# Weight casts moved to GpSimd inside attention's steps, with two weight loads ordered behind the queries' transfers

## Chip, cores and metric

The kernel runs on one core of one Trainium2 chip. The metric is the device time of one execution in microseconds; the time before is the median of three executions.

## What is computed

A trunk of two decoder layers over one sequence of 512 tokens, width 1024, in float32. Layer 0 mixes tokens in chunks of 128 with a gated MLP; then one shared key/value projection is made. Layer 1 is sliding-window attention over these keys and values, with 16 query heads of 64 in 4 groups, a linear distance bias and a learned sink per head. Each layer is followed by a gated MLP of width 2816 with a causal convolution of width 3 and by a gated embedding. The part around the change is this:

```python
q = (xn @ w_q).reshape(B, nb, BLOCK, N_KV_HEADS, GQA_GROUP, HEAD_DIM)
scores = einsum('bnikgd,bnjkd->bnkgij', q, kblk) * (HEAD_DIM ** -0.5)
scores = scores - slopes[:, :, None, None] * dist
scores = where(valid[None, :, None, None], scores, -inf)
m = maximum(max(scores, axis=-1, keepdims=True), sink)
e = exp(scores - m)
probs = e / (sum(e, axis=-1, keepdims=True) + exp(sink - m))
out = einsum('bnkgij,bnjkd->bnikgd', probs, vblk)
return out.reshape(B, S, N_Q_HEADS * HEAD_DIM) @ w_o
```

`kblk` and `vblk` hold, for each block of 128 queries, the previous and the current block of 128 keys.

## The kernel before, in words

Activations lie transposed, features on partitions and tokens along the row. Every float32 product with a weight is made of three matmuls on rounded halves: high x high, high x low, low x high (`mm3`, lines 181 to 183). So each weight is split before use. `plan` writes down the weights in the order of use as *pieces*; a piece of 2048 columns has two *units* of 1024. `load` (line 129) issues a piece's DMA on SyncE's queue into a raw buffer. `pump` makes units ready: ScalarE rounds the raw unit into the high half `wh` (line 154), VectorE subtracts it from the raw one into the low half `wl` (line 155). Both halves have four buffers (`WBUFS`), so a unit's cast waits until TensorE has read the unit four places earlier. During attention there is one raw buffer (`state["tags"] = [0]`), so a piece's load waits for the subtraction of the piece before.

The order of the pieces here is: half of the key/value weight, query weight 0, the other half, query weights 1 to 3, output weights 0 to 3, and then the second MLP.

Attention runs in 16 steps, group g of heads by block n of queries, as a pipeline over a loop `i`: `scores(i)`, the filling work of the step (`fill`), `mix(i-2)`, `turn(i-1)`, `weights(i)`.

- `scores` (lines 774 to 793): two matmuls per head give the scores; VectorE folds the two key blocks with a predicated copy (784) and reduces them with the bias to an exponent and its extreme (788); GpSimd puts the sink into the last column (774); ScalarE takes the four exponentials and their sums (793).
- `weights` (801 to 807): VectorE's reciprocal; one head is scaled by VectorE (807), three by ScalarE (805).
- `turn` (822, 252, 253, 830): TensorE transposes the four heads, ScalarE and VectorE split the result into halves, and GpSimd's affine selects keep the part that belongs to the previous block.
- `mix` (844 to 857): the products with the values; ScalarE and VectorE add the two halves, ScalarE rounds the output (856), GpSimd subtracts for its low half (857).
- `fill` takes from the table `beside`: in steps 0 to 9 the projections of query groups 1 to 3 (`project`), then parts of the output projection (`merge`), and in some steps `more`, which pumps one unit ahead. Steps 0, 1, 3, 4, 6, 7, 10 and 11 have it.

`queries` scales a projected group, splits it (ScalarE at 657, VectorE at 658) and, for the groups 1 to 3, moves the halves into place with four DMAs on SyncE's queue (661, 662), as each half of the partitions has to hold the other side's data.

The order of instructions on each engine is the framework's: a scheduler takes them by priority as they become ready in its own estimate, with `scores`, `turn` and `weights` at high priority. Engines and DMA queues then work strictly in that order. So an instruction that waits holds back what stands behind it on its engine.

Of the kernel before, what the change touches and what calls it, by code (L numbers as in the profile page):

```python
# [8 lines left out]
F32 = mybir.dt.float32  # L9
# [39 lines left out]
def tile_yoco(ctx: ExitStack, tc: tile.TileContext, t, out: bass.AP, out_b: bass.AP):  # L49
    nc = tc.nc  # L50
# [14 lines left out]
    pieces, paired = [], set()  # L65

    def plan(ap_, n, cols, own=None):

        if own and len(own) > 1:
            m = n // len(own)  # L70
            cuts = [(q * m, m) for q in range(len(own))]
        else:
            m = n if n <= UNIT else (n // cols + 1) // 2 * cols
            cuts = [(0, m), (m, n - m)] if m < n else [(0, n)]
        pieces.append((ap_, n, cuts, own))

    def plan_cols(w, n_chunks, kk, cols=256, k0=0):
        for c in range(n_chunks):
            plan(w[c, :, k0 * cols : (k0 + kk) * cols], kk * cols, cols)
# [6 lines left out]
    def plan_ffn(l):  # L86
        for i, (j0, j1) in enumerate(PARTS):
            if i == 0:
                plan_cols(t["w_up"][l], j1, KD)
            else:  # L90
                plan_cols(t["w_up"][l, j0 + 1 : j1], j1 - j0 - 1, KD)
            if i + 1 < len(PARTS):
                plan_cols(t["w_up"][l, j1 : j1 + 1], 1, KD)
            else:
                plan(t["pT"][l], 2 * S, S, own=[(mp, "m4", "m5")])
                plan_cols(t["w_pin"][l], 2, 4)
            plan_cols(t["w_down"][l], 4, j1 - j0, k0=j0)
# [9 lines left out]
    plan_cols(t["w_q"][0:1], 1, KD)  # L107
    plan_cols(t["w_kv"][1:2], 1, KD)
    plan_cols(t["w_q"][1:4], 3, KD)
    plan_cols(t["w_o"], 4, KD)  # L110
    plan_ffn(1)
    free = [j % SLOTS for j in range(NJ, NJ + 8)]
# [4 lines left out]

    units = [(i, q, lo, n) for i, p in enumerate(pieces) for q, (lo, n) in enumerate(p[2])]
    raws, ready = {}, {}
    state = {"raw": 0, "unit": 0, "next": 0, "tags": [0, 1, 2], "turn": 0, "pt": 0}  # L120

    def load(upto, queue=nc.sync):
        while state["raw"] < min(upto, len(pieces)):
            j = state["raw"]
            a, m = pieces[j][:2]
            tags = state["tags"]
            r = wp.tile([P, 2 * UNIT], F32, tag=f"r{tags[state['turn'] % len(tags)]}", bufs=1, name=f"wraw{j}")
            state["turn"] += 1
            queue.dma_start(r[:, :m].rearrange("p (c m) -> p c m", c=2) if j in paired else r[:, :m], a)
            raws[j] = r  # L130
            state["raw"] += 1

    def pump(upto):
        while state["unit"] < min(upto, len(units)):
            i, q, lo, n = units[state["unit"]]
            load(i + 1)
            u = state["unit"]
            own = pieces[i][3]
            if own:
                pool, *tags = own[q]  # L140
                wh, wl = (pool.tile([P, n], F32R, tag=tg, name=f"own{u}_{tg}") for tg in tags)
            else:
                wh = wp.tile([P, UNIT], F32R, tag="wh", bufs=WBUFS, name=f"wh{u}")
                wl = wp.tile([P, UNIT], F32R, tag="wl", bufs=WBUFS, name=f"wl{u}")
            if i in paired:
                whole = raws[i][:, : pieces[i][1]].rearrange("p (c k n) -> p k c n", c=2, n=256)
                src = whole[:, lo // S : (lo + n) // S]
                hi, low = (x[:, :n].rearrange("p (k c n) -> p k c n", c=2, n=256) for x in (wh, wl))
            else:
                src, hi, low = raws[i][:, lo : lo + n], wh[:, :n], wl[:, :n]  # L150
            if u == 0:
                nc.vector.tensor_copy(hi, src)
            else:
                nc.scalar.copy(hi, src)  # L154
            nc.vector.tensor_sub(low, src, hi.bitcast(F32))  # L155
            ready[u] = (wh, wl, n)
            state["unit"] += 1
# [41 lines left out]
    def v(name, i):  # L199
        c = VEC[name] + i  # L200
        return vec[:, c : c + 1]
# [61 lines left out]
    class Norm:  # L263
# [25 lines left out]
        def turn(self):  # L289

            sq = tp.tile([P, S], F32, tag="sq", name=f"{self.name}turn")
            nc.vector.transpose(sq, self.acc)
            self.quarter = const.tile([P, S // 32], F32, tag="quarter", bufs=1, name=f"{self.name}quarter")
            nc.vector.tensor_reduce(self.quarter, sq.rearrange("p (b f) -> p b f", f=32),
                                    axis=mybir.AxisListType.X, op=ALU.add)
# [48 lines left out]
    def gain(name, l=0):  # L344
        return lambda k: v(name, l * KD + k)
# [215 lines left out]
    for c in range(4):  # L561
# [4 lines left out]
        for j in range(2):  # L566
            m = 2 * c + j
# [14 lines left out]
            hi = ap.tile([P, S], F32R, tag=f"ah{m}", name=f"ush{m}")  # L582
# [58 lines left out]
    def queries(ps, g, j):  # L641


        qf = tp.tile([P, S], F32, tag="sq", name=f"qf{g}_{j}")
        m = 2 * g + j
        nc.vector.scalar_tensor_tensor(qf, ps, qscale[:, m : m + 1], rstd, op0=ALU.mult, op1=ALU.mult)
        res = [tp.tile([P, S], F32R, tag=("hs", "sg", "c0", "c1")[2 * j + e], name=f"q{g}_{j}_{e}")
               for e in range(2)]
        if g == 0:
            for e, q in enumerate(res):  # L650
                me, it = sides[e], sides[1 - e]
                nc.scalar.copy(q[me, :], qf[me, :])
                nc.vector.tensor_sub(q[it, :], qf[me, :], q[me, :].bitcast(F32))
            return res

        hi = tp.tile([P, S], F32, tag="acc", name=f"qhi{g}_{j}")
        nc.scalar.copy(hi.bitcast(F32R), qf)
        nc.vector.tensor_sub(qf.bitcast(F32R), qf, hi)
        for e, q in enumerate(res):
            me, it = sides[e], sides[1 - e]  # L660
            nc.sync.dma_start(q[me, :].bitcast(F32), hi[me, :])
            nc.sync.dma_start(q[it, :].bitcast(F32), qf[me, :])
        return res

    qs = {0: []}
    for j in range(2):
        qs[0] += queries(qps[j], 0, j)
# [87 lines left out]
    def fill(i):  # L755
        for f, *args in beside.get(i, []):
            f(*args)
# [9 lines left out]
    def scores(i):  # L767


        g, n = steps[i]  # L770
        nk = 2 * P if n else P
        t0 = (n - 1) * P if n else 0
        pr = prs[:, i % 2]
        nc.gpsimd.tensor_copy(pr[:, :, P], nsink[:, GQ * g : GQ * (g + 1)])
        neg = at.tile([P, GQ], F32, tag="neg", bufs=2, name=f"neg{i}")
        for b in range(2):
            sc = psum(f"sc{i}_{b}").rearrange("p (e h k) -> p e h k", e=2, h=2)
            for j in range(2):
                o = sc[:, j].rearrange("p h k -> p (h k)")[:, :nk]
                q = qs[g][2 * b + j][:, n * P : (n + 1) * P]  # L780
                nc.tensor.matmul(o, q, kh[g // 2][:, g % 2, t0 : t0 + nk], start=True, stop=False)
                nc.tensor.matmul(o, q, kl[g // 2][:, g % 2, t0 : t0 + nk], start=False, stop=True)
            if n:
                nc.vector.copy_predicated(sc[:, :, 0, :], both(own.bitcast(mybir.dt.int32)), sc[:, :, 1, :])
            for j in range(2):
                e = 2 * b + j
                hd = GQ * g + e
                nc.vector.tensor_tensor_reduce(out=pr[:, e, :P], in0=far if n else near, in1=sc[:, j, 0, :],
                                               scale=-slope(hd), scalar=nsink[:, hd : hd + 1],
                                               op0=ALU.add, op1=ALU.min, accum_out=neg[:, e : e + 1])  # L790
        sm = at.tile([P, GQ], F32, tag="sm", bufs=2, name=f"sm{i}")
        for e in range(GQ):
            nc.scalar.activation(pr[:, e, :], pr[:, e, :], AF.Exp, bias=neg[:, e : e + 1], scale=-1.0,
                                 accum_out=sm[:, e : e + 1])
        live[i] = (pr, sm)
# [63 lines left out]
    last = len(steps)  # L859
# [2 lines left out]
    state["tags"] = [0]  # L862
    pts4 = wp.tile([P, 4, S], F32R, tag="r1", bufs=1, name="pts4")
    for i in range(last + 2):
        if i < last:
            with tc.high_priority():
                scores(i)
        if i <= last:
            fill(i)
        if i >= 2:  # L870
            mix(i - 2)
        if i > last:
            fill(i)
        if 0 <= i - 1 < last:
            with tc.high_priority():
                turn(i - 1)
        if i < last:
            with tc.high_priority():
                weights(i)
    state["tags"] = [0, 1, 2]  # L880
    nf = Norm("nf1", [(xp, "x", gain("norm_ffn", 1))])
    for c in range(4):
        for m in (2 * c, 2 * c + 1):
# [226 lines left out]
```

## Time and profile before

| | before |
|---|---|
| median of 3 executions | 1141.46 us (1141.1 to 1141.71) |
| profiled execution | 1141.22 us, of which the span is 1139.5 |
| TensorE busy | 1127.0 us (99%) |
| VectorE busy | 749.6 us (66%) |
| ScalarE busy | 530.0 us (47%) |
| GpSimd busy | 107.7 us (9%) |
| granted TensorE clock | 0.998 |
| casts of line 154 on ScalarE | 197, 202.0 us in all, 1028 ns each |

Busy shares are means over all stages; attention's steps lie between about 591 and 688 us of the span. In the timelines a row gives the start, the duration, the engine, the line, the operation with its output and inputs, and in brackets how long the engine stood idle before and who ended that. PE is TensorE, ACT ScalarE, DVE VectorE, POOL GpSimd, SPq the queue of SyncE.

### The profile page before, as it was taken

The numbers are of one execution on the slowest core, as the hardware profiler recorded it, in microseconds if no ns is written. First come the engines' busy times: TensorE is split into PE (matmuls) and PEld (weight loads), VectorE is DVE, ScalarE is ACT, GpSimd is POOL, SyncE is SP. The second block draws the span as 40 slices with busy tenths as digits, with TensorE's granted clock in tenths as the row PEclk, the third lists the DMA queues.
The fourth block names the chain that finished last, engine by engine and source line by source line (L and its number), as shares of the span: only waits on it lengthen the run. The fifth ranks groups of instructions, "written<-read, shape, count | busy, mean of one in ns | idle before, by whom it ended". The sixth has DMA issues, their size and how long they took to land.

```text
span 1139.5 us, 13604 instructions
## 1 busy us (share of the span) xinstructions
PE 1127.0 (99%) x5266; PEld 940.5 (83%) x5266; DVE 749.6 (66%) x1158; ACT 530.0 (47%) x875; POOL 107.7 (9%) x175
## 2 busy tenths in 40 slices
PE   9999999999999999999999999999999999999997
PEld 7888888888888888888898878888888888888896
DVE  7366477763677367557988977777636763675675
ACT  6533344441344234445657985444313432355562
POOL 2000200000000000021213343000000000000222
PEclk9999999999999999999999999999999999999999
DMA  8422323223223322432224315223223233224302
GB/s 298 145 83 74 111 75 111 101 85 111 78 98 102 111 76 86 134 107 79 74 75 129 93 38 185 98 88 111 78 107 110 66 102 111 93 80 160 111 1 75
DMA packets 25776, 115.41 MB, mean 101 GB/s; under 512 B 2920, under 2 KB 8176, under 8 KB 16240
## 3 DMA queue, kind: packets, MB, share of 16 engines
q1 hardware_dynamic: 25152, 113.89, 29.8%
q8 instruction: 41, 0.67, 0.2%
q10 hardware_dynamic: 560, 0.66, 0.2%
q14 instruction: 23, 0.19, 0.1%
HBM read 108.24 MB, written 2.11 MB: 97 GB/s over the span
## 4 chain that ended last, share of the span: by engine, by line
PE 95%; DVE 2%; issue 1%; ACT 1%; DMA 1%; POOL 0%; SPq 0%; POOLq 0%; DVEq 0%; ACTq 0%
PE up L181 14%; PE up L183 14%; PE up L182 14%; PE d L183 8%; PE d L181 8%; PE d L182 8%; PE gate L181 2%; PE gate L183 2%; PE gate L182 2%; PE u L182 1%; PE u L183 1%; PE u L181 1%; PE o L182 1%; PE o L181 1%; PE o L183 1%; PE q L181 1%
## 5 line engine op out<-in xcount | busy, mean ns | idle before, releaser
L154 ACT CAST wh<-wraw 128x1024 fp32r<-128x1024 f32 (+2 forms) x197 | 202.0, 1028 | 264.6 <-PE d L182 131.0
L155 DVE TENSOR_TENSOR wl<-wraw,wh 128x1024 fp32r<-128x1024 f32 (+1 forms) x198 | 238.4, 1205 | 127.9 <-ACT wh L154 127.6
L181 PE MATMUL up<-nf00h,wh 128*128 128x512 f32 x352 | 137.1, 390 | 0.0
L181 PE MATMUL up<-nf10h,wh 128*128 128x512 f32 x352 | 137.0, 389 | 0.0
L182 PE MATMUL up<-nf00l,wh 128*128 128x512 f32 x352 | 136.9, 389 | 0.0
L183 PE MATMUL up<-nf00h,wl 128*128 128x512 f32 x352 | 136.9, 389 | 0.0
L183 PE MATMUL up<-nf10h,wl 128*128 128x512 f32 x352 | 136.9, 389 | 0.0
L182 PE MATMUL up<-nf10l,wh 128*128 128x512 f32 x352 | 136.9, 389 | 0.0
L181 PE MATMUL d<-ah,wh 128*128 128x512 f32 x352 | 136.9, 389 | 0.0
L182 PE MATMUL d<-al,wh 128*128 128x512 f32 x352 | 136.9, 389 | 0.0
L183 PE MATMUL d<-ah,wl 128*128 128x512 f32 x352 | 136.9, 389 | 0.0
L379 ACT ACTIVATE c<-hs,vec 128x512 f32<-128x512 f32 x88 | 71.5, 815 | 72.0 <-DVE hs L375 71.2
L380 DVE SCALAR_TENSOR_TENSOR c<-hs,vec,c 128x511 f32<-128x511 f32 x88 | 65.8, 749 | 34.5 <-ACT c L379 34.4
L355 DVE TENSOR_TENSOR h<-h,d 128x512 f32<-128x512 f32 x56 | 38.4, 686 | 73.8 <-PE d L183 73.8
L252 ACT CAST ah<-a 128x512 fp32r<-128x512 f32 x44 | 27.4, 622 | 109.5 <-DVE a L385 109.4
L183 PEld LDWEIGHTS up<-nf10h,wl 128*128 128x128 f32 x352 | 66.1, 188 | 13.8
L182 PEld LDWEIGHTS d<-al,wh 128*128 128x128 f32 x352 | 66.1, 188 | 13.8
L183 PEld LDWEIGHTS up<-nf00h,wl 128*128 128x128 f32 x352 | 66.1, 188 | 13.8
L183 PEld LDWEIGHTS d<-ah,wl 128*128 128x128 f32 x352 | 66.1, 188 | 13.7
L182 PEld LDWEIGHTS up<-nf00l,wh 128*128 128x128 f32 x352 | 66.1, 188 | 13.7
L182 PEld LDWEIGHTS up<-nf10l,wh 128*128 128x128 f32 x352 | 66.1, 188 | 13.7
L181 PEld LDWEIGHTS d<-ah,wh 128*128 128x128 f32 x352 | 66.1, 188 | 13.6
(454 smaller groups left out, 2061.7 us busy)
## 6 DMA issues: line engine op xcount, KB each, us to landing
wraw<-in_w_up SPq DMA_DIRECT2D x44, 1024.0 KB, 4.8
wraw<-in_w_down SPq DMA_DIRECT2D x16, 896.0 KB, 4.6
wraw<-in_w_down SPq DMA_DIRECT2D x8, 1024.0 KB, 4.8
wraw<-in_w_gate SPq DMA_DIRECT2D x8, 1024.0 KB, 4.8
wraw<-in_w_u SPq DMA_DIRECT2D x4, 1024.0 KB, 5.9
wraw<-in_w_out SPq DMA_DIRECT2D x4, 1024.0 KB, 4.8
wraw<-in_w_q SPq DMA_DIRECT2D x4, 1024.0 KB, 4.9
wraw<-in_w_o SPq DMA_DIRECT2D x4, 1024.0 KB, 4.9
```

What stands on the lines that cost most here:

```text
L154: nc.scalar.copy(hi, src)
L155: nc.vector.tensor_sub(low, src, hi.bitcast(F32))
L181: nc.tensor.matmul(ps, wh[:, a:b], xh, start=st, stop=False)
L182: nc.tensor.matmul(ps, wh[:, a:b], xl, start=False, stop=False)
L183: nc.tensor.matmul(ps, wl[:, a:b], xh, start=False, stop=en)
L252: nc.scalar.copy(hi, src)
L355: nc.vector.tensor_add(h[m], h[m], ps)
L379: nc.scalar.activation(c, hs, AF.Identity, bias=v("conv_b", l * 2 * NJ + col), scale=cw[2])
L380: nc.vector.scalar_tensor_tensor(c[:, 1:], hs[:, : S - 1], cw[1], c[:, 1:], op0=ALU.mult, op1=ALU.add)
```

## The change

Inside the loop over attention's steps the function that makes the high half of a weight unit is chosen by the step: GpSimd's copy for the steps 1 to 14, ScalarE's in all others. `pump` calls whatever is set when it asks for the unit.

Also, the DMAs of a query group's second half (`j` of 1) are kept for the groups 2 and 3, and the load of the piece `outs + g - 1`, which is output weight 1 or 2, is given an edge behind them. The edge orders the instructions in SyncE's queue; it adds no semaphore.

```diff
+    outs = len(pieces)
     plan_cols(t["w_o"], 4, KD)
...
+    def behind(ins, front):
+        tc.add_manual_dep(ins.ins, front.ins.name,
+                          mybir.DependencyInfo(mybir.DependencyClass.NoSync, mybir.DependencyReason.DATA),
+                          reason="order")
...
-            queue.dma_start(r[:, :m].rearrange("p (c m) -> p c m", c=2) if j in paired else r[:, :m], a)
+            ins = queue.dma_start(r[:, :m].rearrange("p (c m) -> p c m", c=2) if j in paired else r[:, :m], a)
+            for front in state["sent"].pop(j, []):
+                behind(ins, front)
...
-                nc.scalar.copy(hi, src)
+                state["cast"](hi, src)
             nc.vector.tensor_sub(low, src, hi.bitcast(F32))
...
-            nc.sync.dma_start(q[me, :].bitcast(F32), hi[me, :])
-            nc.sync.dma_start(q[it, :].bitcast(F32), qf[me, :])
+            sent = [nc.sync.dma_start(q[me, :].bitcast(F32), hi[me, :]),
+                    nc.sync.dma_start(q[it, :].bitcast(F32), qf[me, :])]
+            if g > 1 and j:
+                state["sent"].setdefault(outs + g - 1, []).extend(sent)
...
     for i in range(last + 2):
+        state["cast"] = nc.gpsimd.tensor_copy if 0 < i < last - 1 else nc.scalar.copy
         if i < last:
...
     state["tags"] = [0, 1, 2]
+    state["cast"] = nc.scalar.copy
```

More of the change, by code (lines that the diff above doesn't have):

```diff
@@ L119, in tile_yoco @@
     raws, ready = {}, {}
-    state = {"raw": 0, "unit": 0, "next": 0, "tags": [0, 1, 2], "turn": 0, "pt": 0}
+    state = {"raw": 0, "unit": 0, "next": 0, "tags": [0, 1, 2], "turn": 0, "pt": 0, "sent": {}, "cast": nc.scalar.copy}
+    def behind(ins, front):
+        tc.add_manual_dep(ins.ins, front.ins.name,
+                          mybir.DependencyInfo(mybir.DependencyClass.NoSync, mybir.DependencyReason.DATA),
+                          reason="order")
     def load(upto, queue=nc.sync):
```

## The prediction

> **What bounds the kernel now.** I read the page first, then busy time by stretches of the attention, then the waits of TensorE and VectorE there, then the timelines of the engines around each wait, and last the chain of waits.
>
> ```profile
> span 1139.5 us, 13604 instructions
> PE 1127.0 (99%) x5266; PEld 940.5 (83%) x5266; DVE 749.6 (66%) x1158; ACT 530.0 (47%) x875; POOL 107.7 (9%) x175
> ```
>
> TensorE is busy for 1127.0 of 1139.5 us: all that any edit can return without taking matmuls away is 12.5 us, most of it at the two ends. The change acts in attention's sixteen steps, so I cut them where TensorE's idle time changes.
>
> ```profile
> core 0: us, PE busy (x) PEld busy (x) DVE busy (x) ACT busy (x) POOL busy (x), PEclk, DMA share, GB/s
> 603.00:649.50 46.50, 46.50 (x256) 39.76 (x254) 40.13 (x129) 39.99 (x126) 15.73 (x33) 1.00 0.43 123
> 649.50:662.50 13.00, 10.54 (x59) 7.77 (x58) 12.51 (x49) 12.77 (x48) 5.85 (x14) 1.00 0.25 50
> 662.50:669.50 7.00, 7.00 (x37) 5.60 (x35) 4.80 (x18) 5.87 (x20) 3.35 (x8) 1.00 0.32 135
> 669.50:684.30 14.80, 13.59 (x66) 10.55 (x66) 10.12 (x32) 10.56 (x35) 6.04 (x10) 1.00 0.00 1
> ```
>
> Up to 649.5 TensorE never stands: the queries' projections fill every step, and whatever ScalarE saves there is hidden. From 649.5 to 662.5 TensorE stands 13.00 - 10.54 = 2.46 us, with ScalarE (12.77 of 13) and VectorE (12.51) both full and GpSimd at 5.85. In the last stretch it stands 1.21 us. So 3.67 us of idle is what the change can reach. The stops in the middle stretch:
>
> ```profile
> 649.50 0.39 PE L844 MATMUL pv<-pts,vt 128*128 128x512 f32 x1
> 650.68 0.41 PE L822 MATMUL tr<-ident,prs 128*128 128x128 f32 x2 [0.80 <-DVE prs L807]
> ...
> 660.90 0.49 PE L181 MATMUL o<-oh,wh 128*128 128x512 f32 x1
> 662.11 0.50 PE L182 MATMUL o<-ol,wh 128*128 128x512 f32 x1 [0.71 <-POOL ol L857]
> ...
> PE tr L822 <- DVE prs L807: 1.7, 3, 0.8
> ...
> 652.52 0.23 PE o L181
> ```
>
> The first four rows are the first and the last stop (the bracket is the idle time and who ended it), the fifth is from TensorE's waits (us in total, times, longest), the last from the chain. That one says that a 512-wide matmul holds TensorE for 0.23 us when work follows; a bar of 0.39 contains 0.16 of draining. A stop therefore costs more from start to start than its idle time: 650.68 - 649.50 - 0.23 = 0.95 us for the first, 662.11 - 660.90 - 0.23 = 0.98 for the last. There are four: three transposes that wait for VectorE's scaling, 1.7 + 3 x 0.16 = 2.2 us together, and a projection that waits for GpSimd's low half of the output, 0.98.
>
> **The change part by part.** (a) The casts. Line 154 runs on ScalarE seven times in the steps that precede the stops:
>
> ```profile
> L154 ACT CAST wh<-wraw x7: 1032/1038/1052, 599.4 to 646.9; 128x1024 fp32r<-128x1024 f32 x7
> ...
> 642.93 0.95 ACT wh L154
> 643.90 1.23 DVE wl L155
> ```
>
> By the order in which steps ask for units, these seven are the second half of the third query weight, both halves of the fourth, and both halves of the first two output weights; all are asked for in steps 1 to 11, so all seven move. They take 0.95 us each of ScalarE's queue (the chain's row; 1.04 is the bar), 6.65 us in all. The first five lie further back under TensorE's full stretch, where nothing that ScalarE gains shows. The last two, which end at 643.9 and begin at 646.9 (1.9 us), feed the stops. The first of them is on the chain: VectorE's subtraction at 643.90 waits for it.
>
> What VectorE loses to ScalarE there, between 640 and 663, is the whole of one answer:
>
> ```profile
> DVE wl L155 <- ACT wh L154: 0.6, 1, 0.6
> DVE ds L801 <- ACT prs L793: 0.3, 1, 0.3
> DVE pts L253 <- ACT pts L252: 0.3, 1, 0.3
> DVE side L852 <- ACT side L848: 0.2, 1, 0.2
> ```
>
> 1.4 us. VectorE has no other slack before 662, so the three transposes can come earlier by at most 1.4 of their 2.2 us, however idle ScalarE becomes. I take all 1.4, because ScalarE is relieved of 1.9 us in the ten microseconds where these waits lie. The bounds are 0.6 (only the wait for the cast itself goes) and 1.4; late next is VectorE's own work.
>
> The fourth stop hangs on ScalarE and GpSimd:
>
> ```profile
> 659.68 0.60 ACT p11h L252
> 660.39 1.09 POOL pts L830
> 661.64 0.43 POOL ol L857
> ```
>
> The chain runs from ScalarE's cast of the turned probabilities, in a queue without a gap, to GpSimd. If ScalarE arrives 1.9 us sooner, less the 1.4 by which TensorE itself moved, and the select is no longer stretched by the subtraction beside it, the 0.98 goes. Bounds: 0 and 0.98; I take 0.98.
>
> What GpSimd pays: the trace has no 128x1024 cast on it. The nearest rows by width and by operation:
>
> ```profile
> L542 POOL TENSOR_SCALAR_AFFINE_SELECT wsT<-wsT 128x1024 f32<-128x1024 f32 x1 | 1.1, 1091 | 20.3 <-DMA wsT<-in_wsT 20.3
> ...
> 590.88 0.24 POOL L687 CAST diff<-vd 128x64 fp32r<-128x64 f32 x1 [16.82 <-DVE vd L708]
> 600.33 1.59 POOL L687 CAST diff<-vd 128x64 fp32r<-128x64 f32 x3 [0.41 <-DVE vd L708]
> ...
> 600.42 1.23 DVE L155 TENSOR_TENSOR wl<-wraw,wh 128x1024 fp32r<-128x1024 f32 x1
> ```
>
> Same width and one input: 1.09 us; it is the nearest, and I take it. Sixteen 64-wide casts at 0.24 would be 3.8, which counts the start sixteen times over: the upper end. Seven at 1.09 are 7.6 us on an engine that is busy for 15.73 + 5.85 + 3.35 + 6.04 = 31.0 of 81.3 us in these steps; it has room, but its queue is in order, so place matters. The last two rows show three casts that should take 0.7 taking 1.59 while VectorE subtracts weights: the two engines shut each other out. It goes the other way too:
>
> ```profile
> 540.94 1.34 POOL L282 TENSOR_TENSOR n1acc<-n1acc,n1sq 128x512 f32<-128x512 f32 x1 [4.06 <-ACT n1sq L277]
> 541.05 2.32 DVE L155 TENSOR_TENSOR wl<-wraw,wh 128x1024 fp32r<-128x1024 f32 x1
> ```
>
> A subtraction that takes 1.23 takes 2.32 behind a GpSimd instruction: up to 1.1 us per cast, taken from the very engine that bounds the stretch. [...]
>
> When would the two casts run? Each needs the buffer that the fourth query weight leaves, and the last matmuls that read its halves start at
>
> ```profile
> 640.51 0.39 PE L183 MATMUL q<-n11h,wl 128*128 128x512 f32 x1
> 645.57 0.39 PE L183 MATMUL q<-n11h,wl 128*128 128x512 f32 x1
> ```
>
> so they run from about 641 and 646. Beside the first, VectorE scales once and adds from PSUM; beside the second it reduces scores from PSUM. [...] I charge 0.2 us for both; bounds 0 and 2.2.
>
> (b) The held loads. SyncE's queue before:
>
> ```profile
> 610.91 1.10 SPq L661 DMA_DIRECT2D q<-qhi  x2
> 612.06 1.23 SPq L662 DMA_DIRECT2D q<-qf  x2
> 613.33 0.59 SPq L129 DMA_DIRECT2D wraw<-in_w_o  x1
> ...
> 631.71 1.10 SPq L662 DMA_DIRECT2D q<-qf  x2
> 633.39 0.33 SPq L129 DMA_DIRECT2D wraw<-in_w_o  x1
> ...
> 651.77 1.10 SPq L662 DMA_DIRECT2D q<-qf  x2
> 661.02 0.33 SPq L129 DMA_DIRECT2D wraw<-in_w_o  x1
> ```
>
> The two loads concerned are those at 633.39 and 661.02, and they stand behind the third and fourth queries' transfers already (631.71 and 651.77). By itself this part changes no order and costs nothing; it keeps a load, which now could be asked for sooner, from standing in SyncE's queue in front of transfers that the scores wait for. Behind each held load only later loads queue.
>
> Sum: -1.4 - 0.98 + 0.2 = -2.2 us. The profiled execution took 1141.22 us (span 1139.5 and 1.7 around it); it would be 1139.0. The median of three is 1141.46, 0.24 above it, so the forecast for the median is 1139.3. The instruction order on each engine is recomputed by the framework when costs move; the trace can't show that. It can add up to the rest of the idle time or take as much.
>
> **The rivals.** *GpSimd's queue and lock decide.* The selects of step 7 and the matmul that needs them:
>
> ```profile
> 646.42 0.64 POOL L830 TENSOR_SCALAR_AFFINE_SELECT u7l<-pts 128x512 fp32r<-128x512 f32 x1
> 647.89 0.39 PE L844 MATMUL pv<-u7l,diff 128*128 128x512 f32 x1
> ```
>
> There is 647.89 - 647.06 = 0.83 us of slack. A cast of 1.09 put in front makes it 0.3 late; one that also waits out a VectorE subtraction (0.9 more, the 600.33 row) makes it 1.1 late, and it then holds the subtraction back by 1.1. Twice, at steps 9 and 10, that is 2 x (1.1 + 1.1) = 4.4, less the 1.9 that ScalarE still gains: +2.5, or 1144.0 us. It decides from the point where cast and lock together exceed 0.83 us in front of a select. For it: VectorE is 96% full there, and a cast is longer than any GpSimd instruction now in that stretch uncontended. [...]
>
> *A load that isn't held.* The first output weight's load (613.33) is not among the held ones. It waits for the subtraction of the fourth query weight's second half, and both halves' casts now move. If they are two casts (2 x 1.09 = 2.2 us) later and the load comes to stand in front of the second query's transfers, these begin at 613.33 + 2.2 instead of 610.91, 4.6 us later, and the fifth step's scores need them. What of this the distance to that step covers I leave open: between 0 and 4.6 us, and I take the middle, 2.3, which eats the gain of 2.2: 1141.6 us (1143.9 at the upper end). Against it: the load stands 2.4 us behind those transfers now.
>
> *Nothing arrives.* VectorE takes back what ScalarE gives, or the casts and subtractions are queued just as late as now: 1141.5 us.
>
> **How the numbers follow.** About 0.2% (2.3 us) is what a measurement of this kernel can tell from no change. The forecast's mechanism gets 0.58. Its centre, 2.2, lies at that bound; reordering has more idle time left to take (3.67 and the draining, 0.16 a stop) than to give back, so I split it 0.46 faster by more, 0.12 within. GpSimd's queue gets 0.27: 0.25 slower by more and 0.02 within. The unheld load gets 0.08: its upper end 0.05 slower, its middle 0.03 within. Nothing arrives 0.07, all within. Sums: faster 0.46, same 0.24, slower 0.30. The range goes down to 4.7 us of gain (3.67 idle plus six stops' draining), 1136.8 (1141.46 - 4.7), and up to the queue's price, 1144.0; 0.05 is left out below, 0.13 above.
>
> **What would show it.** Right: seven 128x1024 casts on GpSimd near 1.1 us; no line 154 on ScalarE between 600 and 650; VectorE's waits for ScalarE between 640 and 663 near zero; TensorE's idle time before 662 down from 2.46 to about 1; the transposes' stops still for VectorE. Wrong: casts over 2 us; weight subtractions of 2 us in the steps; TensorE waiting for selects or low halves by GpSimd; scores that wait for a query's transfer; or a first stretch that is no longer full, since the whole argument takes 603 to 649.5 as closed.

## The result: slower, and by a way that the prediction had left aside

The changed kernel takes 1144.86 us (median of 7, 1144.26 to 1145.67) against 1141.10 (1141.02 to 1141.74) for the kernel before on the same chip: ratio 1.0032, 95% interval 1.0021 to 1.0042. It is 3.8 us slower. The forecast was 1139.3 us, with a range from 1136.8 to 1144.0.

The profiled execution took 1144.86 us. From the top of its page (lines carry the changed kernel's numbers from here on: the scaling, 807 before, is 818, the query's low half 667, the weight's low half 164):

```profile
span 1143.1 us, 13598 instructions
PE 1129.7 (99%) x5266; PEld 941.2 (82%) x5266; DVE 750.4 (66%) x1158; ACT 524.4 (46%) x868; POOL 118.8 (10%) x182
```

TensorE does the same 5266 matmuls and is busy for 2.7 us more than before (1129.7 against 1127.0); only the other 0.9 us of the span, longer by 3.6, is idle time. So a part of the loss lies in matmuls that run more slowly. The stretches at the same cuts as in the prediction, and one cut of their own (span, then busy time and count of each engine, the granted clock, DMA):

```profile
603.00:649.50 46.50, 46.50 (x256) 39.71 (x254) 40.73 (x129) 34.82 (x120) 25.47 (x44) 1.00 0.44 125
649.50:662.50 13.00, 9.94 (x46) 6.93 (x45) 11.44 (x44) 12.04 (x45) 6.15 (x12) 0.92 0.42 122
662.50:669.50 7.00, 7.00 (x35) 5.75 (x35) 4.90 (x16) 4.80 (x15) 2.90 (x4) 0.90 0.00 0
669.50:684.30 14.80, 13.43 (x66) 9.79 (x65) 9.83 (x36) 11.49 (x42) 6.26 (x13) 1.00 0.01 3
...
658.90:664.00 5.10, 4.99 (x16) 3.48 (x16) 3.44 (x13) 4.43 (x17) 2.43 (x7) 0.67 0.49 193
```

The first stretch is as closed as before: ScalarE has 5 us less to do there and TensorE never stands. From 649.5 to 662.5 TensorE now stands 3.06 us (2.46 before), and between 658.9 and 664.0 the granted clock is 0.67, where it was 1.00: 5.1 x 0.33 = 1.7 us of slow matmuls. About 1 us of the longer busy time is left unassigned. TensorE's waits (us in total, times, longest) and the rows behind the new one, then two rows of the kernel before:

```profile
PE tr L833 <- DVE prs L818: 1.5, 2, 0.8
PE sc L792 <- DMA q<-qf: 1.5, 1, 1.5
...
649.14 0.17 DVE L812 RECIPROCAL ds<-sm 128x4 f32<-128x4 f32 x1
649.22 1.23 DVE L164 TENSOR_TENSOR wl<-wraw,wh 128x1024 fp32r<-128x1024 f32 x1
650.38 0.47 DVE L818 TENSOR_SCALAR prs<-prs,ds 128x128 f32<-128x128 f32 x1
...
655.64 0.68 DVE L667 TENSOR_TENSOR qf<-qf,qhi 128x512 fp32r<-128x512 f32 x1
...
656.35 1.10 SPq L671 DMA_DIRECT2D q<-qf  x2
657.55 0.54 SPq L136 DMA_DIRECT2D wraw<-in_w_o  x1
...
658.68 0.30 PE L792 MATMUL sc<-kh,q 128*128 128x128 f32 x1 [1.47 <-DMA q<-qf]
```

```profile
651.06 0.68 DVE L658 TENSOR_TENSOR qf<-qf,qhi 128x512 fp32r<-128x512 f32 x1
...
659.77 1.23 DVE L155 TENSOR_TENSOR wl<-wraw,wh 128x1024 fp32r<-128x1024 f32 x1
```

Many rows stand elsewhere on VectorE than before; two catch the eye. The subtraction that makes `wl` of output weight 1's second half was at 659.77 and is now at 649.22, in front of the scaling of step 9's probabilities (steps count from 0; the expectations of g1 and g4 call it step 10's); and the query's low half, L667, was at 651.06 and is now at 655.64. Its transfer left SyncE at 651.77 and leaves now at 656.35, and step 12's scores wait 1.47 us for it. The clock falls behind that stop, which ends at 658.68: it is 1.00 up to 660.4 and 0.50 from 660.5 to 663.8.

### The profile page after: what moved, and what is told of

The parts are those of the page before. It is cut to its first block, busy times and chain, and to the rows that moved or that the text cites. A ratio compares the mean times of both kernels' runs of the same rounds, so it can differ in the third digit from the quotient of the medians.

```text
span 1143.1 us, 13598 instructions
## 1 busy us (share of the span) xinstructions
PE 1129.7 (99%) x5266; PEld 941.2 (82%) x5266; DVE 750.4 (66%) x1158; ACT 524.4 (46%) x868; POOL 118.8 (10%) x182
## 4 chain that ended last, share of the span: by engine, by line
PE 90%; DVE 4%; ACT 2%; issue 1%; POOL 1%; DMA 1%; SPq 0%; POOLq 0%; DVEq 0%; ACTq 0%
PE up L190 14%; PE up L192 14%; PE up L191 14%; PE d L191 8%; PE d L192 8%; PE d L190 8%; PE gate L190 2%; PE gate L191 2%; PE gate L192 2%; PE u L191 1%; PE u L190 1%; PE u L192 1%; PE o L191 1%; PE o L192 1%; PE o L190 1%
## 5 line engine op out<-in xcount | busy, mean ns | idle before, releaser
L163 ACT CAST wh<-wraw 128x1024 fp32r<-128x1024 f32 (+2 forms) x190 | 194.7, 1027 | 267.9 <-PE d L191 131.3
L190 PEld LDWEIGHTS up<-nf00h,wh 128*128 128x128 f32 x352 | 66.1, 188 | 13.7
```

What stands on the lines that cost most here:

```text
L163: state["cast"](hi, src)
L190: nc.tensor.matmul(ps, wh[:, a:b], xh, start=st, stop=False)
```

## The experiments

The candidates: the framework's **new instruction order** costs the time; the **casts** do, through GpSimd's queue and through the time by which GpSimd and VectorE stretch each other's instructions (2.32 us for a subtraction of 1.23 in the prediction's rows), there called the lock; the **held loads** do. Letters for theories in an expectation belong to its own round. Each kernel was timed against the kernel before on its own chip; the medians of before there lie between 1141.22 and 1141.5. So a few tenths of a microsecond between kernels of different rounds are not to be relied on.

**First round: one thing back at a time, the order free to move again.**

e1: the changed kernel, and the low half's subtraction bound ahead of that `wl`.

```
+            sub = nc.vector.tensor_sub(low, src, hi.bitcast(F32))
+            for front in state["split"].pop((i, q), []):
+                behind(sub, front)
...
+        low = nc.vector.tensor_sub(qf.bitcast(F32R), qf, hi)
+        if g == 3 and j:
+            state["split"].setdefault((outs + g - 2, 1), []).append(low)
```

> The changed kernel, with one more edge: on VectorE the subtraction that makes the second half of the second output weight's low half stands behind the subtraction that makes the last query's low half. All seven casts stay on GpSimd. Theory A (the query's subtraction was queued behind weight and step work, so its transfers left 4.6 us late and the scores waited 1.47 us, after which TensorE's clock fell): the wait for the transfer is gone, the granted clock stays 1.00 from 649.5 to 669.5, and the time is 1139 to 1141.5 us. Theory B (GpSimd's casts themselves cost it, by the lock against VectorE and by the queue in front of selects): the casts are all there, so it stays at 1144 to 1145 us.

Measured 1143.15 us, ratio 1.0014 (1.0005 to 1.0023); about half of the loss is gone, and no more; it lies in neither theory's range. The wait for the transfer is gone and the clock is at 1.00, but others have come:

```profile
PE pv L859 <- ACT prs L820: 1.4, 1, 1.4
PE tr L837 <- DVE prs L822: 1.2, 1, 1.2
PE o L192 <- ACT oh L871: 0.7, 2, 0.5
```

e2: the casts alone, no load held (`if g > 1 and j` made `if False`).

> The changed kernel without the held loads: casts on GpSimd alone. SyncE's queue then has the two output weights' loads in front of the transfers of the third and fourth queries' second halves; every other engine's order is that of the changed kernel. Theory A: the loads wait for subtractions that are over by 634.7 and 650.5, so little is lost: 1144.5 to 1146 us. If the edges on the loads are the harm, it is near 1141 us.

1144.92 us, 1.0031 (1.0019 to 1.0042): as the changed kernel, with the wait for the transfer as long (1.5 us). The held loads fall as the cause of the loss. What they are worth in the old order was not run.

e4: GpSimd casts in steps 1 to 7 only (`if 0 < i < 8`).

> The changed kernel with GpSimd's casts in steps 1 to 7 alone: five casts move, the two of the second output weight stay on ScalarE. Theory A: VectorE's order then has the query's subtraction ahead of that weight's second one, as before the change; no wait for a transfer, clock 1.00, 1140 to 1141.5 us, since the first five casts lie under a full TensorE. Theory B: five sevenths of the harm remain, about 1143.8 us.

1143.25 us, 1.0016 (1.0007 to 1.0025). VectorE's order around the query's low half is that of before, and still it is slower, with longer waits for GpSimd's `ol` (1.5 us, 0.7 before) and `oh` (0.7, 0.3 before) and a new one for `p13l` (1.0); for the scaling TensorE waits 1.7 us, as before. By its number it lies nearer to theory B; f1 below, with all seven casts on GpSimd and no loss, speaks against that theory.

e5: the changed kernel with seven 512-wide products that nothing reads in front of the waiting scores.

> The changed kernel with seven more 512-wide matmuls (0.23 us each, 1.6 in all) in front of the scores that wait for the transfer; their product is overwritten by the scores. They fill TensorE's stop and lengthen nothing else much. Theory A with the clock as a part of its own: the scores start as late as in the changed kernel, but the clock stays at 1.00 and the nine matmuls that took 0.42 us take 0.23, so about 1143 us. If the clock's fall is no consequence of that stop, or costs nothing: 1144.5 to 1145.5 us.

1144.46 us, 1.0028 (1.0018 to 1.0038), clock at 1.00. Its later waits moved as well (the scores wait 1.5 us for `p13l`), so it does not part the clock from the stop.

e1, e4 and e5 have one fault: each edit lets the framework order the steps anew, so the time mixes what was edited with another order. (e2 keeps the changed kernel's.) So the order had to be held.

**Second round: the order held.** An edge from each instruction to the one that is to be issued ahead of it on its engine fixes the order within each engine, and nothing between engines.

```
+    kept = {i.name: i for i in nc.cur_bb.bb.instructions}
+    for runs in ORDER.values():          # per engine: another kernel's order
+        names = [f"I-{n}" for a, b in runs for n in range(a, b)]
+        for front, ins in zip(names, names[1:]):
+            tc.add_manual_dep(kept[ins], front, ...)    # as in behind(): order only
```

f1 and f2 with the kernel before and the changed one make a square: order by engine of the casts.

> The seven casts stay on GpSimd and the held loads stay, but from the first k product to the last o product every engine is bound to the order of instructions that the kernel before has (779 of TensorE, 253 of VectorE, 226 of ScalarE, 101 of GpSimd, 40 of SyncE; only the casts are free to lie where GpSimd can take them). Theory A (the loss comes from the new order, not from GpSimd): at or below the kernel before, 1139.3 to 1141.5 us; no stop of TensorE for the transfer of a query, granted clock 1.00 between 649 and 670, and the stops between 649.5 and 662.5 at 2.5 us or less against 3.06 in the changed kernel. Theory B (the lock between VectorE and GpSimd, or GpSimd's queue in front of its subtractions and selects, makes the loss): 1143 us or more, with stops for VectorE's scaling or for GpSimd's ol that are longer than before's.

> The opposite corner: all casts on ScalarE as in the kernel before, the held loads in, and every engine bound to the order that the changed kernel has between the first k product and the last o product; only the seven casts are free to lie where ScalarE can take them. Theory A: the loss is there without a cast on GpSimd, 1144 to 1146 us (ScalarE's casts can add to it), with a stop of about 1.5 us for the transfer of the query behind which the clock falls. Theory B: 1141 to 1142 us.

| | casts on ScalarE | casts on GpSimd |
|---|---|---|
| order of before | 1141.22 (before) | 1140.56, ratio 0.9993 (0.9984 to 1.0002) |
| order of the changed kernel | 1145.99, 1.0045 (1.0032 to 1.0057) | 1144.86, 1.0032 (changed kernel) |

The order costs 4.8 us with the casts on ScalarE and 4.3 with the casts on GpSimd. Moving the casts gains 0.7 and 1.1 in the medians, whichever order stands; the interval of the first reaches past 1, so it is not clear of no gain. The new order is the cause, and the casts are not. f1's and f2's middle stretch:

```profile
649.50:662.50 13.00, 11.35 (x63) 8.46 (x62) 12.50 (x51) 12.66 (x48) 5.68 (x13) 1.00 0.25 52
649.50:662.50 13.00, 9.40 (x45) 6.66 (x44) 12.14 (x44) 12.53 (x47) 5.80 (x12) 0.94 0.35 96
```

f2 has the 1.5 us wait for the query's transfer and the lower clock (0.94 here, 0.87 from 662.5 to 669.5) without one cast on GpSimd.

f7 and f8 hold one engine each to the order of before and let the others follow.

> The changed kernel with VectorE alone bound to the order of the kernel before (253 instructions between the first k and the last o product); the other engines take what follows from it. TensorE's order still differs from the kernel before's at 33 places, ScalarE's at 47, GpSimd's at 8. If VectorE's order is what costs, 1141.5 us or less, and no stop for a query's transfer. If TensorE's own order costs as much as VectorE's, 1142 to 1143.5 us.

> The reverse: TensorE alone is bound to the order of the kernel before (779 instructions), VectorE's order differs from it at 88 places, ScalarE's at 87, GpSimd's at 28. If VectorE's order is what costs, 1143.5 to 1146 us with a stop for the query's transfer of 1 us or more. If TensorE's order is what costs, 1141.5 us or less.

f7: 1139.94 us, 0.9987 (0.9978 to 0.9996). f8: 1147.48 us, 1.0052 (1.0039 to 1.0064). With VectorE's order alone back the whole loss is gone, though the other engines' orders still differ from before's. f8 missed its range: TensorE's order alone back does not help. It does not price that order by itself, since the framework made yet another order for VectorE (88 places off before's). f7 first, then f8:

```profile
649.50:662.50 13.00, 12.13 (x67) 9.52 (x67) 11.84 (x46) 12.03 (x46) 6.01 (x13) 1.00 0.31 82
PE o L190 <- ACT oh L867: 0.6, 1, 0.6
PE pv L855 <- ACT prs L804: 0.5, 1, 0.5
```

```profile
649.50:662.50 13.00, 9.38 (x43) 6.91 (x42) 11.47 (x45) 11.90 (x44) 6.27 (x13) 0.88 0.42 121
PE sc L792 <- DVE neg L799: 1.9, 1, 1.9
PE tr L833 <- DVE prs L818: 1.5, 2, 0.8
```

In f7 TensorE stands 0.87 us where it stood 2.46, and its waits no longer name a scaling. f7 is also the fastest version, clear of both kernels: the change, with VectorE's order kept. f8's longest stop is for a reduction (`neg`), not for the transfer that was expected.

f6: f1 with the first five casts back on ScalarE.

> As f1_old_order, but the first five casts are back on ScalarE at the places that the kernel before gives them; only the two casts of output weight 1 are on GpSimd. If the prediction's step holds that the first five are worth nothing because TensorE has no idle time there, this is as fast as f1_old_order, 1140.3 to 1140.9 us, and its first stop for a transpose after 649 us is gone as there. If the gain comes from all seven, it is about 1141.0 to 1141.3 us.

1140.53 us, 0.9992 (0.9983 to 1.0001), against f1's 1140.56. With the order held, the five casts under the full TensorE are worth nothing that can be told from the noise, as the prediction said.

f4: f1 with rows moved by hand at two of TensorE's remaining stops.

> As f1_old_order, with two things moved by hand: in steps 9, 10 and 11 VectorE's scaling of the probabilities stands ahead of the reduction that lay between it and the reciprocal (0.24 us each), and GpSimd's subtractions for two o operands stand ahead of two selects of step 11. If TensorE's remaining stops hang on these two rows, two stops for transposes get 0.2 us shorter each and the 0.97 us stop of an o product shrinks to 0.3 us or less: 1139.3 to 1140.0 us. If the selects that are now later are waited for, the gain is eaten and it is 1140.3 us or more.

1140.04 us, 0.9988 (0.9979 to 0.9997): some 0.5 below f1, just above what was expected at best. The stop of the `o` product went from 0.97 us to 0.32 (from start to start, less the 0.23 of a product); of the two transposes one got shorter (0.78 to 0.37), the other longer (0.71 to 0.88, its own wait now for a reduction).

**Third round: single rows of VectorE's order.** Both start from f1.

> f1_old_order (casts on GpSimd, the order of the kernel before on every engine) with one row of VectorE moved to where the changed kernel has it: the 1.23 us subtraction that makes wl of output weight 1's second half stands between step 10's reciprocal and its scaling instead of 9 us later. If this row is what the new order costs, the scaling, step 10's transposes and all that VectorE does behind it come about 1.2 us later, the query's low half too: 1141.4 to 1142.4 us against 1140.6, a stop for the transposes at 649.7 of about 1 us, and a short one or none for the query's transfer. If the row is harmless by itself, 1140.3 to 1140.9 us.

> f1_old_order with the other row moved: the subtraction of the query's low half stands behind step 10's second scaling, about 4 us later, as in the changed kernel; wl stays where the kernel before has it. If the late transfer is what costs, TensorE stops for it 1 to 1.6 us in step 12's scores and the granted clock falls behind that: 1142 to 1144 us. If TensorE's other work covers it (fewer stops ahead of it than in the changed kernel), 1140.3 to 1141.5 us with the clock at 1.00; a stop of 1 us or more with the clock at 1.00 would say that the stop alone doesn't make it fall.

g1, `wl` ahead of the scaling: 1140.24 us, 0.9991 (0.9982 to 1.0000). The most conspicuous row of the new order is harmless by itself. g2, the query's low half late: 1143.21 us (1140.97 to 1145.18), 1.0017 (1.0008 to 1.0026). One row out of place costs 2.65 us over f1.

```profile
654.20 0.68 DVE L667 TENSOR_TENSOR qf<-qf,qhi 128x512 fp32r<-128x512 f32 x1
...
654.91 1.10 SPq L671 DMA_DIRECT2D q<-qf  x2
...
657.23 0.44 PE L792 MATMUL sc<-kh,q 128*128 128x128 f32 x1 [1.26 <-DMA q<-qf]
...
656.00:660.00 4.00, 2.77 (x8) 2.39 (x9) 3.69 (x16) 3.42 (x14) 1.47 (x3) 0.61 0.31 70
660.00:664.00 4.00, 4.00 (x17) 3.51 (x17) 1.69 (x4) 1.52 (x7) 0.80 (x3) 0.54 0.40 119
```

g3 puts the seven unread products into that stop, every order held.

> g2_low_late (one row of VectorE moved: the query's low half 4 us later, everything else in the order of the kernel before) with seven extra 512-wide products on TensorE, which nothing reads, in the place where it waits for the late transfer (7 x 0.23 = 1.6 us, as long as the stop). If most of what that row costs is the clock behind the stop, the clock stays at 1.00 and the time is 1140.9 to 1141.9 us, with 0.3 to 1.3 us left over f1_old_order for the stop itself. If the stop and the lateness cost it, 1142.7 to 1143.7 us as in g2_low_late, with the clock at 1.00.

1141.15 us (1140.52 to 1141.78), 0.9998 (0.9990 to 1.0007).

```profile
655.35 1.86 PE L792 MATMUL sc<-kh 128*128 128x512 f32 x7
657.05 0.22 PE L796 MATMUL sc<-kh,q 128*128 128x128 f32 x1
...
649.50:662.50 13.00, 12.27 (x69) 9.73 (x68) 11.51 (x40) 11.66 (x45) 4.77 (x12) 1.00 0.24 54
662.50:669.50 7.00, 6.79 (x36) 5.46 (x34) 5.29 (x21) 6.34 (x21) 3.19 (x8) 1.00 0.32 129
```

The scores begin as late as in g2 (657.05 against 657.23), but the clock holds at 1.00 in both stretches, where g2 has 0.78 and 0.91. Of the 2.65 us that the late row costs, 2.06 go with the clock behind the stop, and 0.59 are left for the stop and the lateness (0.42 if each kernel is taken against its own before).

g4: the changed kernel's order on all engines, with only this row back.

> The changed kernel's order on every engine, with one row of VectorE put back: the subtraction of the query's low half directly behind step 10's first scaling, some 4.6 us earlier. If that row is the larger part of the loss (2.65 us as g2_low_late has it), 1141.8 to 1142.8 us, with the clock at 1.00 and no stop for the transfer; what is left over f1_old_order, 1.2 to 2.2 us, is then the rest of the new order. If the other rows of the order cost as much again, 1143 us or more.

1145.74 us, 1.0039 (1.0026 to 1.0053): a clear miss. The wait for the transfer is gone, and another one stands 2 us further on:

```profile
660.43 0.50 PE L190 MATMUL o<-oh,wh 128*128 128x512 f32 x1 [1.59 <-ACT oh L867]
```

It could have been read in the changed kernel. Its chain of waits (start, us, what) runs past the late transfer and not through it:

```profile
649.31 1.15 DVE wl L164
650.46 0.40 DVE prs L818
...
657.52 1.65 ACT prs L804 x8
659.17 0.27 ACT oh L867
...
659.48 0.51 PE o L190
```

Up to 652.4 it lies on VectorE, through the early `wl`; from 652.8 on it is ScalarE's queue, whose exponentials and then `oh` release the `o` products at 659.44, only 0.8 us after the transfer released the scores. So the late low half is enough for a loss of 2.65 us in the old order but isn't the only late row of the new one: with it cured, `oh` is waited for instead. Putting all of VectorE's order back, f7, gains 4.9 us. Which of the other rows weighs how much is left open; the early `wl`, harmless in g1, is on the chain here.

## Why the prediction was wrong, step by step

- **The step that failed** is the sentence that the order "is recomputed by the framework" and "can add up to the rest of the idle time or take as much". It stood behind the sum, was priced at the idle time that the trace shows, and got no chance of its own. Where it did enter the chances, it counted as a likely gain. It measured +4.3 us (changed kernel over f1), more than all the idle time it was measured against (3.67), since matmuls behind a stop can run slowly too (0.42 us for 0.23 in the changed kernel). The forecast was one for a fixed order, 1139.3; f1 has that order and takes 1140.56, f7, with VectorE's order alone fixed, 1139.94.
- **-1.4 for VectorE's waits for ScalarE.** The size was too large, and the mechanism shows only with the order held. In f1 these waits between 640 and 663 fall from 1.4 to 0.6 us (in the changed kernel they are 2.0):

```profile
DVE ds L812 <- ACT prs L804: 0.3, 1, 0.3
DVE pts L262 <- ACT pts L261: 0.3, 1, 0.3
...
PE tr L833 <- DVE prs L818: 1.0, 2, 0.5
PE o L191 <- POOL ol L868: 0.7, 1, 0.7
```

  Of three transposes that waited, the first no longer does; its stop was 0.95 us. The median gains 0.7, which is not clear of the noise.
- **-0.98 for the wait for `ol`.** Nothing of it came in f1 (0.7 then and now), because in the old order the select still stands beside a weight subtraction and takes 1.09 us, where f1's other selects from 645 to 663 take 0.63 or 0.64:

```profile
659.27 1.23 DVE L164 TENSOR_TENSOR wl<-wraw,wh 128x1024 fp32r<-128x1024 f32 x1
...
659.90 1.09 POOL L841 TENSOR_SCALAR_AFFINE_SELECT pts<-p11h 128x512 fp32r<-128x512 f32 x1 [2.03 <-ACT p11h L261]
```

  In g1, where this `wl` is gone from there, the stop is 0.51 us (from start to start, less the 0.23 of a product), where f1 has 0.97. So the stretching subtraction was named rightly; that it would go was not followed through.
- **The cast at 1.09 us** was right: 1.03 to 1.05 in six of seven.

```profile
609.31 1.23 DVE L164 TENSOR_TENSOR wl<-wraw,wh 128x1024 fp32r<-128x1024 f32 x1 [1.48 <-POOL wh L163]
...
609.35 2.09 POOL L163 CAST wh<-wraw 128x1024 fp32r<-128x1024 f32 x1
642.20 1.03 POOL L163 CAST wh<-wraw 128x1024 fp32r<-128x1024 f32 x1
...
642.33 0.99 DVE L818 TENSOR_SCALAR prs<-prs,ds 128x128 f32<-128x128 f32 x1
```

- **The lock** is there as stretched instructions: a cast beside a subtraction took 2.09 us, and a scaling beside a cast 0.99, where one alone took 0.28. No run shows the 0.2 us that the sum charges for the last two casts. In the changed kernel the scaling beside the first (642.20) took 0.7 longer; beside the second (647.20) the reductions and the addition, which read PSUM, took their usual 0.33 and 0.42. But that scaling lies in the first stretch, where TensorE never stands. The rival built on GpSimd's queue and lock had the sign right and the mechanism wrong: its 1144.0 is near the result by luck, for f1 has the same casts and no loss.
- **The rival of the load that isn't held** did not come: the load stayed behind the second query's transfers.

```profile
613.33 1.10 SPq L671 DMA_DIRECT2D q<-qf  x2
614.53 0.53 SPq L136 DMA_DIRECT2D wraw<-in_w_o  x1
```

- **The five casts, and the held loads, at nothing:** the casts right with the order held (f6), the loads in the changed kernel's order (e2). But "changes no order" was meant of SyncE alone. That moving the five casts alone, with the order free, costs 1.8 us over before (e4) was outside the argument.
- **What was listed as a sign of being wrong** included scores that wait for a query's transfer; this is the sign that came. In the lower bound, 3.67 and six times 0.16 are 4.6 us, not 4.7; the bound stays 1136.8.

## What to carry to other kernels

Where a framework orders the instructions, a change has two effects: what it moves, and the new order. Price them apart, and compare the order of rows on the bounding engine in both traces before any mechanism is believed; an experiment that leaves the order free mixes both again. Where the order before is known to be good, keep it with the change: here keeping VectorE's turned 3.8 us of loss into 1.5 us of gain.

When one late row is found, look along the chain for the next that is late by nearly as much before counting on its cure.

## What the hardware showed that was not expected

A stop of TensorE of 1.3 to 1.5 us can be followed by some microseconds at nearly half its speed. In the changed kernel the stop takes 1.47 us and the clock is 0.57 from 660 to 664; `o` products then start 0.42 us apart instead of 0.23. In g2 the stop takes 1.26, and granted clocks of 0.61 and 0.54 stand in the two stretches of 4 us from 656 to 664 (the stop ends at 657.23).

```profile
662.20 0.63 PE L190 MATMUL o<-oh,wh 128*128 128x512 f32 x1
662.62 0.63 PE L191 MATMUL o<-ol,wh 128*128 128x512 f32 x1
```

That the stop brings the low clock is shown by g2 (0.78 and 0.91 in the two stretches from 649.5 to 669.5) against g3, which fills it (1.00 in both). In g2 this cost 2.06 us, more than three times what was left for the stop itself. It does not come every time: g2's runs spread from 1140.97 to 1145.18 us, those of f1 and g3 from 1140.0 to 1141.8, and the profiled executions of e1, e5 and g4 have stops of 1.4, 1.5 and 1.59 us with the clock at 1.00. What decides is not shown. The row that brings a stop of 1.26 us cost 2.65 us here, and seven unread matmuls in the stop were cheaper than the silence (1141.15 us against 1143.21).
